# One transformer layer on one core: the MLP's late operand combinations, the second residual and the last row normalization placed elsewhere

## The chip, the cores and the metric

The kernel runs on one core of one Trainium2 chip. The metric is the device time of one execution in microseconds; a time for a kernel is the median of its runs. The profile is one execution, taken by the hardware profiler. Engines are called PE (TensorE), DVE (VectorE), ACT (ScalarE), POOL (GpSimd) and SP (SyncE, whose queue starts most DMAs).

## The reference

One layer of a decoder trunk in float32, with 1024 tokens and a model width of 1024. The first half (token mixing: an HGRN2 branch and a retention branch, merged and projected by `w_o`) is left out here, since the change does not touch it. What follows it:

```python
x = _layer_norm(ALPHA * x + (1 + gate1) * y, ln1_g, ln1_b)       # y: output of w_o
u = x * (1 + scale2) + shift2
h = square(relu(u @ w_up + b_up))                                # 1024 x 4096
y = h @ w_down + b_down                                          # 1024 x 1024
x = _layer_norm(ALPHA * x + (1 + gate2) * y, ln2_g, ln2_b)       # the output
```

`_layer_norm` takes mean and variance over the 1024 columns of a row, normalizes, multiplies by a per-column scale and adds a per-column shift.

## The kernel before

Every float32 matmul is made of three (`mm3`, lines 186 to 188): both operands are split into a high and a low part, and high·high, high·low and low·high are added up in PSUM. A split (`split`, lines 180 to 182) is one ACT copy for the high part and one DVE subtraction for the low part, so each operand costs both engines an operation.

The large products use Strassen's scheme in Winograd's form: a 2x2 block product from seven block products and not eight. Its right-hand combinations for the up projection are T1 to T4, made from the four blocks B11, B12, B21, B22 of `u` (`combos`, line 402): T1 = B12 - B11, T3 = B22 - B12, T2 = B22 - T1, T4 = B21 - T2, computed in place in the float32 blocks (T4 in a tile of its own, tag "tf"), and each split into two tiles of the pool "U" (14 tiles, all in use at this point). Its left-hand combinations S1 to S4 are made from the weights as these are loaded (`specs_S`, line 216; the DVE sums are line 227).

The stages that the change touches, in order:

1. The output projection (`out_proj`, line 1243). For each of eight tiles of 128 tokens: two column halves of 24 matmuls each, then residual and statistics on DVE, `pow` on POOL for the inverse deviation, normalization on ACT (line 1303). One tile later, `out_second` (line 1315) transposes the normalized tile by PE, writes `u`, and makes the second residual `zp = z * RA + RB` (lines 1331 and 1332, 128 x 1024, on DVE), which POOL's queue stores to memory (`z2_d`).
2. `up_plain` (line 1381): the first group of 256 hidden units as four plain products of 24 matmuls, with its outputs squared, combined by DVE and stored from a pool of four "relu" tiles.
3. `combos`, run to its end: T1, then the subtractions for T3, T2, T4, then the splits of T2, T3, T4.
4. `seven` (line 440): the other 15 groups, seven products of 12 matmuls each, in the order A11·B11, S1·T1, S2·T2, S4·B22, S3·T3, the next group's A12·B21, A22·T4. Results leave PSUM through tiles of a pool "e" (14 buffers). `use_square` (line 1350) makes the left-hand combinations of the down projection out of them; POOL's queue stores these (line 1348).
5. `down_seven` (line 1390): the down projection as four stages of 16 steps. A step's operands are split up to five steps ahead (`prepare`). When a piece of 128 x 512 of the output is complete, `first_part` (line 1456) multiplies it by the gate row, adds the second residual (loaded back from `z2_d` by SP into one of three "zp" tiles) and takes the statistics; when both halves of a row tile are there, `second_part` (line 1465) applies mean, deviation, scale and shift in two three-operand DVE operations for each half and stores the half. Row tiles 0 to 3 and the upper halves of 4 to 7 are complete before the last stage is done; the lower halves of 4 to 7 come out of PSUM one after the other at the very end (lines 1493 to 1500).

The order of the instructions on an engine is not the order of the program text. A planner runs the whole program against its own cost estimates and puts next on each engine the instruction that is ready and stands earliest in the text. So a move in the text changes a rank, and an instruction is passed by others while it is not ready. Pools of tiles are laid out like stacks from the left and the right end of the on-chip memory; a pool that opens where another was closed waits until that one's tiles are released.

## Time and profile before

| | us |
|---|---|
| median of 3 runs | 2324.97 |
| lowest, highest | 2318.06, 2326.09 |
| the profiled execution | 2319.84 |
| its span, first to last instruction | 2318.1 |
| PE busy | 2250.6 (97%) |
| DVE busy | 1652.0 (71%) |
| ACT busy | 1008.7 (44%) |
| POOL busy | 294.6 (13%) |
| mean granted clock of PE | 0.994 |

Busy shares are means over stages with different limits. A row of the timeline has a start, a duration, the engine, the line, the operation and the tiles (written <- read), and in brackets the idle time before it with what ended it; rows of operations in a run are merged (x2). A row of the busy time by stretch has the stretch, its length, busy time and instructions for each engine, the granted clock of PE, the DMA share and GB/s. A row of the groups has the line, engine, operation, tiles, shapes and count, then the busy time and the mean of one in ns, then the idle time before them. A row of a single line's instructions has the shortest, median and longest duration in ns, and the first and the last start.

### The profile page before, as it was taken

How to read it: one execution, taken by the hardware profiler on the slowest of the kernel's cores; microseconds unless marked ns; L12 is line 12 of the kernel's file. 1: busy time of each engine (PE TensorE's matmuls, PEld its weight loads, DVE VectorE, ACT ScalarE, POOL GpSimd, SP SyncE). 2: the span in 40 equal slices, each digit the busy share in tenths (PEclk: the TensorE clock that was granted, in tenths of full speed). 3: DMA queues.
4: the chain of work that ended last, by engine and by line, in shares of the span. 5: the costliest groups of instructions: out<-in, count | busy, mean ns of one | idle time of the engine just before them, and what ended most of it. 6: DMA issues, size and time to landing. Idle time of an engine off the chain costs nothing.

```text
span 2318.1 us, 29884 instructions
## 1 busy us (share of the span) xinstructions
PE 2250.6 (97%) x10366; PEld 1851.3 (80%) x10366; DVE 1652.0 (71%) x3078; ACT 1008.7 (44%) x1829; POOL 294.6 (13%) x460
## 2 busy tenths in 40 slices
PE   6999999999999999999989999999989999999997
PEld 5888888888888788778877788888878888788886
DVE  7866768676777556778876667667886666668669
ACT  4433435443333352432435556222465555643441
POOL 0111010111111120010011222013012111100001
PEclk9999999999999999999999999999999999999999
DMA  9676655433333441122234666864244444777653
GB/s 287 220 229 219 224 195 200 159 129 108 116 109 112 164 150 60 42 91 63 75 104 156 236 193 211 297 212 154 95 145 164 154 152 152 283 254 241 211 168 127
DMA packets 227415, 385.86 MB, mean 166 GB/s; under 512 B 17480, under 2 KB 122688, under 8 KB 226496
## 3 DMA queue, kind: packets, MB, share of 16 engines
q1 hardware_dynamic: 197232, 285.95, 38.7%
q0 software_dynamic: 29712, 97.55, 11.3%
q8 instruction: 82, 1.34, 0.2%
q14 instruction: 69, 0.57, 0.1%
q10 hardware_dynamic: 320, 0.45, 0.1%
HBM read 282.17 MB, written 101.72 MB: 166 GB/s over the span
## 4 chain that ended last, share of the span: by engine, by line
PE 62%; issue 23%; DVE 6%; DMA 3%; POOL 3%; ACT 2%; SPq 0%; ACTq 0%; POOLq 0%; DVEq 0%
PE psd L187 11%; PE psd L186 11%; PE psd L188 11%; PE psa L188 3%; PE psa L187 3%; PE psa L186 3%; PE psc L187 3%; PE psc L186 3%; PE psc L188 3%; PE psb L1119 2%; PE psc L1105 1%; PE psb L186 1%; PE psb L187 1%; PE psb L188 1%; DVE U L182 1%
## 5 line engine op out<-in xcount | busy, mean ns | idle before, releaser
L186 PE MATMUL psd<-U,wh 128*128 128x512 f32 x760 | 305.1, 403 | 2.1 <-ACT wh L181 1.5
L187 PE MATMUL psd<-U,wh 128*128 128x512 f32 x760 | 303.8, 400 | 1.4 <-DVE U L182 1.4
L188 PE MATMUL psd<-U,wl 128*128 128x512 f32 x760 | 303.4, 399 | 0.0
L181 ACT ACTIVATE bh<-s 128x512 fp32r<-128x512 f32 x204 | 128.3, 633 | 248.3 <-PE psd L187 61.1
L186 PE MATMUL psd<-U,bh 128*128 128x512 f32 x496 | 193.8, 391 | 2.1 <-DVE e L449 2.1
L188 PE MATMUL psd<-U,bl 128*128 128x512 f32 x496 | 193.7, 390 | 0.0
L187 PE MATMUL psd<-U,bh 128*128 128x512 f32 x496 | 193.5, 390 | 0.0
L182 DVE TENSOR_TENSOR bl<-raw,bh 128x512 fp32r<-128x512 f32 x153 | 104.6, 689 | 121.4 <-ACT bh L181 121.2
L181 ACT ACTIVATE bh<-raw 128x512 fp32r<-128x512 f32 x153 | 96.9, 636 | 216.3 <-PE psd L187 88.8
L182 DVE TENSOR_TENSOR bl<-s,bh 128x512 fp32r<-128x512 f32 x204 | 139.4, 687 | 69.1 <-ACT bh L181 69.1
L186 PEld LDWEIGHTS psd<-U,wh 128*128 128x128 f32 x760 | 143.1, 189 | 31.0 <-ACT U L181 1.9
L187 PEld LDWEIGHTS psd<-U,wh 128*128 128x128 f32 x760 | 143.8, 189 | 28.6 <-DVE U L182 2.8
L188 PEld LDWEIGHTS psd<-U,wl 128*128 128x128 f32 x760 | 144.0, 189 | 27.6 <-DVE wl L182 0.4
L181 ACT ACTIVATE wh<-raw 128x512 fp32r<-128x512 f32 (+1 forms) x87 | 61.7, 730 | 200.5 <-PE psd L187 174.0
L181 ACT ACTIVATE U<-hr 128x512 fp32r<-128x512 f32 x112 | 70.6, 630 | 157.2 <-issue 69.3
L186 PEld LDWEIGHTS psd<-U,bh 128*128 128x128 f32 x496 | 93.6, 189 | 22.2 <-DVE e L449 2.8
L188 PEld LDWEIGHTS psd<-U,bl 128*128 128x128 f32 x496 | 93.4, 188 | 19.6
L187 PEld LDWEIGHTS psd<-U,bh 128*128 128x128 f32 x496 | 93.5, 189 | 19.4
L182 DVE TENSOR_TENSOR U<-hr,U 128x512 fp32r<-128x512 f32 x112 | 76.8, 686 | 44.4 <-ACT U L181 44.0
L186 PE MATMUL psa<-U,bh 128*128 128x512 f32 x248 | 97.7, 394 | 4.6 <-ACT bh L181 4.3
L188 PE MATMUL psa<-U,bl 128*128 128x512 f32 x248 | 97.5, 393 | 1.0 <-DVE bl L182 1.0
L187 PE MATMUL psa<-U,bh 128*128 128x512 f32 x248 | 97.4, 393 | 0.0
(404 smaller groups left out, 5578.1 us busy)
## 6 DMA issues: line engine op xcount, KB each, us to landing
raw<-in_w_in SPq DMA_DIRECT2D x146, 512.0 KB
raw<-in_w_down SPq DMA_DIRECT2D x48, 512.0 KB
raw<-in_w_ada SPq DMA_DIRECT2D x32, 512.0 KB
raw<-in_w_up SPq DMA_DIRECT2D x32, 512.0 KB
raw<-in_w_pb SPq DMA_DIRECT2D x20, 512.0 KB
adw<-in_w_ada SPq DMA_DIRECT2D x16, 512.0 KB
v_d<-e POOLq DMA_DIRECT2D x32, 256.0 KB, 4.4
rg_d<-e POOLq DMA_DIRECT2D x32, 256.0 KB, 2.6
```

The source lines that it names most:

```text
L181: self.nc.scalar.activation(hi, src, AF.Copy)
L182: self.nc.vector.tensor_tensor(lo, src, hi.bitcast(F32), op=ALU.subtract)
L186: r = mm(out, wh, uh, start=start, stop=False, skip_group_check=more)
L187: mm(out, wh, ul, start=False, stop=False, skip_group_check=more)
L188: return r, mm(out, wl, uh, start=False, stop=stop, skip_group_check=more)
L1105: mm(G[e], l[:, n % 2, es], r, start=n == 0 and i == 0, stop=i == 2, skip_group_check=n > 0)
L1119: mm(po, l, r, start=i == 0, stop=i == len(pairs) - 1)
```

## The change

Three edits, and what they need of pools.

- Late combinations: `combos` runs only up to T1's split before the first seven-product group begins. The subtractions for T3, T2, T4 and T2's split come in the text behind the products A12·B21, A11·B11 and S1·T1 of that group; T3's and T4's splits behind S2·T2 and S4·B22. The pool of the temporary and of the "relu" tiles stays open until the last group; "relu" tiles (4) now also hold part of the outputs of the seven-product groups, and "e" has 7 buffers for the rest, where it had 14 for all.
- Second residual: the two operations of 128 x 1024 for each row tile go from DVE to POOL.
- Down projection's normalization: in `first_part` the two operations of a piece that is already in SBUF go to POOL (12 of 16 pieces; the four that come straight from PSUM stay on DVE). In `second_part`, row tiles 0 to 3, and the upper halves of 4 to 6, are normalized by ACT (scale and bias per row, the bias made by a small DVE operation); the column scale is multiplied by DVE (tiles 0 to 3) or POOL (4 to 6), the column shift added by POOL. The lower halves of 4 to 6 and all of 7 stay as they were.

```diff
@@ combos
-        t3 = Bf["B12"]
-        sub(t3, Bf["B22"], t3)
-        t2 = Bf["B22"]
+        t3, t2 = Bf["B12"], Bf["B22"]
+        sub(t3, t2, t3)
         sub(t2, t2, t1)
@@ out_second
-        V.tensor_tensor(zp, z, RA, op=ALU.mult)
-        V.tensor_tensor(zp, zp, RB, op=ALU.add)
+        nc.gpsimd.tensor_tensor(zp, z, RA, op=ALU.mult)
+        nc.gpsimd.tensor_tensor(zp, zp, RB, op=ALU.add)
@@ up_plain
+    def rt(self):
+        return self.tp.tile([P, 512], F32, tag="relu", bufs=4, name=self.uid("relu"))
...
-        tile = lambda: self.tp.tile([P, 512], F32, tag="relu", bufs=4, name=self.uid("relu"))
-        use = self.use_square(0, tile, (1, 1))
+        use = self.use_square(0, self.rt, (1, 1))
@@ down_seven
         def first_part(t, cs, bank=None):
...
-            V.tensor_tensor(z, z if bank is None else bank, consts["g2"][:, cs], op=ALU.mult)
             zp = fp.tile([P, 512], F32, tag="zp", bufs=3, name=self.uid("zp"))
             nc.sync.dma_start(zp, self.z2_d[t][:, cs])
-            V.tensor_tensor(z, z, zp, op=ALU.add)
+            E = nc.gpsimd if bank is None else V
+            E.tensor_tensor(z, z if bank is None else bank, consts["g2"][:, cs], op=ALU.mult)
+            E.tensor_tensor(z, z, zp, op=ALU.add)
             V.bn_stats(stats[:, t, 6 * (cs.start // 512):6 * (cs.start // 512) + 6], z)
 
         def second_part(t):
             mv, rs = self.norm_stats(stats[:, t])
+            nm = stats[:, t, 24:25]
+            if t < 7:
+                V.scalar_tensor_tensor(nm, mv[:, 0:1], -1.0, rs, op0=ALU.mult, op1=ALU.mult)
             for cs in (lo, up):
                 z = rows[t][:, cs]
-                V.scalar_tensor_tensor(z, z, mv[:, 0:1], consts["lg"][:, cs], op0=ALU.subtract, op1=ALU.mult)
-                V.scalar_tensor_tensor(z, z, rs, consts["lb"][:, cs], op0=ALU.mult, op1=ALU.add)
+                if t < 4 or t < 7 and cs == up:
+                    nc.scalar.activation(z, z, AF.Identity, scale=rs, bias=nm)
+                    E = V if t < 4 else nc.gpsimd
+                    E.tensor_tensor(z, z, consts["lg"][:, cs], op=ALU.mult)
+                    nc.gpsimd.tensor_tensor(z, z, consts["lb"][:, cs], op=ALU.add)
+                else:
+                    V.scalar_tensor_tensor(z, z, mv[:, 0:1], consts["lg"][:, cs], op0=ALU.subtract, op1=ALU.mult)
+                    V.scalar_tensor_tensor(z, z, rs, consts["lb"][:, cs], op0=ALU.mult, op1=ALU.add)
                 nc.sync.dma_start(self.out[t * P:(t + 1) * P, cs], z)
@@ build
-    ups = [(("up", j), k.use_square(j, k.et, (1, 0))) for j in range(1, 16)]
+    ups = [(("up", j), k.use_square(j, k.rt, (1, 0))) for j in range(1, 16)]
...
-        with ExitStack() as s:
-            k.tp = k.pool("tf", "right", s)
-            drain(k.second_parts(1))
-            k.up_plain()
-            drain(k.combos(k.u2f, k.tp))
+        k.tp = k.pool("tf", "right", sh)
+        drain(k.second_parts(1))
+        k.up_plain()
+        parts = k.combos(k.u2f, k.tp)
+        for _ in range(4):
+            next(parts)
         sw.close()
         k.hp = k.pool("hparts", "left")
         with ExitStack() as se:
             k.ev = k.pool("ev2", "left", se)
-            k.e_bufs = 14
-            drain(k.seven(ups))
+            k.e_bufs = 7
+            body = k.seven(ups)
+            next(body)
+            for _ in range(3):
+                next(parts)
+            next(body)
+            drain(parts)
+            drain(body)
```

## The prediction

> **What bounds the kernel now.** I read the page's head, then the busy time by stage, then the timeline of the stages in which TensorE is not full.
>
> ```profile
> span 2318.1 us, 29884 instructions
> ```
>
> ```profile
> core 0: us, PE busy (x) PEld busy (x) DVE busy (x) ACT busy (x) POOL busy (x), PEclk, DMA share, GB/s
> 1600.00:1700.00 100.00, 99.25 (x470) 82.33 (x469) 82.19 (x124) 54.27 (x104) 10.41 (x19) 1.00 0.32 106
> 1700.00:1800.00 100.00, 94.68 (x406) 77.38 (x405) 71.23 (x103) 58.76 (x93) 18.11 (x34) 0.97 0.47 157
> ...
> 1712.10:1718.90 6.80, 5.76 (x13) 4.11 (x14) 6.42 (x10) 2.97 (x7) 0.54 (x1) 0.52 0.07 8
> 1718.90:1732.50 13.60, 13.60 (x61) 11.24 (x60) 12.37 (x20) 8.49 (x15) 1.95 (x4) 1.00 0.55 183
> ...
> 1998.00:2002.00 4.00, 4.00 (x11) 3.13 (x12) 4.00 (x7) 2.31 (x5) 1.22 (x3) 0.57 0.74 217
> ...
> 2260.00:2318.00 58.00, 45.05 (x199) 36.94 (x197) 54.75 (x102) 5.88 (x10) 7.85 (x8) 0.92 0.37 127
> ```
>
> In the output projection (1600 to 1700) TensorE idles 0.75 us: nothing is to be won there. Just past 1700 it loses 5.3 us and half its clock for a while. From 2260 on VectorE is busy for 54.75 of 58 us, while TensorE has finished after 45.05, at 2305.05; VectorE alone sets the end. So the change touches one stage with slack and two places that count. Profiled time is 2319.84 us, span 2318.1, so 1.74 us lie around the span.
>
> **The gap at 1708, and the late combinations.**
>
> ```profile
> 1712.15 0.80 PE L186 MATMUL psa<-U,bh 128*128 128x512 f32 x1 [4.33 <-ACT bh L181]
> 1718.69 0.40 PE L186 MATMUL psd<-U,bh 128*128 128x512 f32 x1
> 1997.96 0.50 PE L186 MATMUL psd<-U,bh 128*128 128x512 f32 x1 [2.08 <-DVE e L449]
> ```
>
> ```profile
> 1711.47 0.63 ACT L181 ACTIVATE bh<-s 128x512 fp32r<-128x512 f32 x1 [2.59 <-DVE s L227]
> 1713.79 0.60 ACT L437 ACTIVATE e<-psd 128x512 f32<-128x512 f32 x1 [1.69 <-DVE U L182]
> ```
>
> TensorE finishes A11·B11 at 1712.15 - 4.33 = 1707.8 and waits for the weight combination S1, which VectorE reached only after its work on T2, T3 and T4. The second ACT row shows the first evacuation waiting for VectorE's last such split: the buffer pool that follows reuses the temporary's room. The S1·T1 product then runs 1712.15 to 1718.69 at a granted clock of 0.52, 6.5 us; at full speed a product takes 13.60 / 5 = 2.72 (the five behind it, 1718.90 to 1732.50). Loss: 4.3 + 3.8 = 8.1 us, the most that this edit can return.
>
> After it, S1, S2, S4 and S3 stand ahead of the three subtractions, so S1·T1 starts at 1707.8 and ends at 1710.5; the next in program order, S2·T2, needs T2. What is late next is VectorE:
>
> ```profile
> L182 DVE TENSOR_TENSOR U<-U,U 128x1024 fp32r<-128x1024 f32 x10 | 11.8, 1218 | 0.0
> L408 DVE TENSOR_TENSOR U<-U,U 128x1024 f32<-128x1024 f32 x6 | 7.1, 1216 | 0.0
> ```
>
> ```profile
> 1686.19 2.35 DVE L408 TENSOR_TENSOR U<-U,U 128x1024 f32<-128x1024 f32 x2
> 2297.53 1.28 DVE L1462 TENSOR_TENSOR row<-row,zp 128x512 f32<-128x512 f32 x2
> 2313.51 1.41 DVE L1470 SCALAR_TENSOR_TENSOR row<-row,stats,lb 128x512 f32<-128x512 f32 x2
> ```
>
> These pairs give the cost in a queue: 2.35 - 1.22 = 1.13 us for 1024 columns, 1.28 - 0.68 = 0.60 for 512, 1.41 - 0.74 = 0.67 for the three-operand form. From 1686.2 to the first half of T2's low part stand 15 operations of 1024 columns (2 for T1, 4 low parts of B12 and B22, 2 of T1, 6 subtractions, 1 of T2) and 16 of 512 (two weight low parts, four S sums and their low parts, the next group's A12, four of the plain product's output, one sum): 17.0 + 9.6 = 26.6, and 2.3 for a GpSimd lock (below): 1715.1. TensorE can fill with the next group's A12·B21 (to 1713.3) and S4·B22 (to 1716.0). Both fills: no wait, -8.1. One: 1.8 idle. What does such an idle cost? The 2.08 us at 1996 was followed by 4 us at a clock of 0.57, 1.7 us more; so 3.5 in all, -4.6. None: 4.6 idle and 3.8 of slow clock as now, about 0. I take -6.4, midway between the first two, as the planner picks what is ready.
>
> The Trainium skill ("TensorE: Matmul & The Clock Gate", Why this matters for your kernels) warns only of idle gaps beyond about 3 us; by it one fill would leave -6.3 and not -4.6. The 2.08 us row speaks against it, and I go by the row.
>
> Fewer "e" buffers cost nothing in my count: a group now needs six from seven, and four from "relu"; the products of a group, 7 times 2.72 = 19 us, cover the time in which an output waits for its store. Without that cover each late evacuation would stop TensorE.
>
> **Second residual on GpSimd.**
>
> ```profile
> L1331 DVE TENSOR_TENSOR zp<-z,RA x8: 1220/1226/1226, 1610.4 to 1683.8; 128x1024 f32<-128x1024 f32 x8
> ```
>
> ```profile
> 1696.98 0.69 ACT L1358 ACTIVATE relu<-psd,cols 128x512 f32<-128x512 f32 x1 [0.65 <-PE psd L188]
> ```
>
> This multiply and an addition like it leave VectorE, eight times. Now the row of this trace that matters most, GpSimd's 128x512 tensor_tensor in the projection before, first on GpSimd, then what VectorE did beside it:
>
> ```profile
> 1571.46 2.20 POOL L1221 TENSOR_TENSOR U<-U,e 128x512 f32<-128x512 f32 x1 [0.63 <-DVE U L1220]
> 1576.15 1.28 POOL L1221 TENSOR_TENSOR U<-U,e 128x512 f32<-128x512 f32 x1 [2.49 <-DVE U L1220]
> ```
>
> ```profile
> 1571.31 1.21 DVE L182 TENSOR_TENSOR wl<-raw,wh 128x1024 fp32r<-128x1024 f32 x1
> 1572.55 2.19 DVE L182 TENSOR_TENSOR wr<-raw,wr 128x1024 fp32r<-128x1024 f32 x1
> ...
> 1575.99 0.68 DVE L1218 TENSOR_TENSOR U<-U,psd 128x512 f32<-128x512 f32 x1
> 1576.71 1.28 DVE L1220 TENSOR_TENSOR U<-U,e 128x512 f32<-128x512 f32 x1
> ```
>
> Alone it takes 1.28. When a VectorE operation with both inputs in SBUF is running, GpSimd waits for its end (1572.5) and ends at 1573.66; the next VectorE operation of that kind waits for that (1572.55 to 1574.74, 1.1 past GpSimd's end). L1220 likewise ends 0.56 after GpSimd's 1577.43. L1218, with one input in PSUM, keeps its 0.68, and GpSimd keeps its 1.28 beside it. So the two engines exclude each other for operations with two inputs in SBUF: moving one takes 0.60 off VectorE and can block VectorE for 1.14 (1572.52 to 1573.66).
>
> A 1024-column operation on GpSimd has no row. It lies between 1.28 and twice that, 2.6; I take 2.3, near the upper end, for little of the 1.28 is fixed if it goes as VectorE's 0.68 and 1.22. Two per row tile are 4.6 of a period of (1683.8 - 1610.4) / 7 = 10.5 us, on an engine 10% busy (10.41 of 100): hidden under the next tile's 48 matmuls. Only the last tile counts: the multiply (from 1683.8) ends about when T1's subtraction starts at 1686.2, the addition gets in between, and that chain moves by 2.3. T1's subtraction then ends at 1688.5 + 2.3 = 1690.8 and the first half of B12's low part at 1692.0. The third plain product ends at 1696.9 (the ACT row above) and lasts two products, 5.4, so it starts near 1691.5: +0.5, between -0.7 (all the idle time of 1600 to 1700) and +2.3 (all of the shift). The tile's store leaves 2 x 2.3 - 2 x 1.23 = 2.1 us later; pow and the next store queue behind it on GpSimd, the next buffer pool waits for it, and two plain products cover that.
>
> **The normalization of the down projection.**
>
> ```profile
> L1470 DVE SCALAR_TENSOR_TENSOR row<-row,stats,lb 128x512 f32<-128x512 f32 x16 | 11.3, 744 | 0.0
> L1469 DVE SCALAR_TENSOR_TENSOR row<-row,stats,lg 128x512 f32<-128x512 f32 x16 | 11.2, 742 | 0.0
> L1462 DVE TENSOR_TENSOR row<-row,zp 128x512 f32<-128x512 f32 x12 | 7.9, 682 | 0.0
> L1463 DVE BATCH_NORM_STATS2 stats<-row 128x6 f32<-128x512 f32 x12 | 7.9, 681 | 0.0
> L182 DVE TENSOR_TENSOR U<-U,U 128x512 fp32r<-128x512 f32 x8 | 5.5, 684 | 0.0
> L1459 DVE TENSOR_TENSOR row<-row,g 128x512 f32<-128x512 f32 x8 | 5.3, 680 | 0.0
> L182 DVE TENSOR_TENSOR U<-hr,U 128x512 fp32r<-128x512 f32 x7 | 4.6, 661 | 0.0
> ```
>
> ```profile
> L1240 POOL TENSOR_TENSOR stats<-stats,small 128x1 f32<-128x1 f32 x8 | 7.8, 981 | 298.8 <-DVE stats L1239 298.8
> ```
>
> From 2257 VectorE loses 16 operations of the first parts (8 pieces), 16 three-operand ones of rows 0 to 3 against 8 multiplies, and 6 of rows 4 to 6: 9.6 + 10.7 - 4.8 + 4.0 = 19.5 us off. ScalarE gets 11 at 0.63 (the bh row above) = 6.9, beside TensorE's last products. GpSimd gets 16 + 8 + 6 = 30, at 1.28 each 38.4. What counts is what the two share. VectorE keeps 15 splits, 4 zp sums and 8 multiplies at 0.60 and 10 three-operand ones at 0.67 with two inputs in SBUF: 16.2 + 6.7 = 22.9. Together 61.3 us from 2257.2: 2318.5, where VectorE's last operation now ends at 2314.92. So +3.5; each GpSimd operation holds VectorE only 1.14 of its 1.28, and I leave those 4 us for operations that don't fit into one another.
>
> The bounds. Below, no exclusion: then row 7 alone follows TensorE's end, three first-part operations, pow at 0.98 and four three-operand ones, 1.8 + 1.0 + 2.7 = 5.5: 2310.5, -4.4. Above, nothing of GpSimd's work rides under VectorE's: 38.4 - 19.5 = +18.9. What can ride are VectorE's 12 statistics, 8 sums from PSUM and 4 products from PSUM, 24 x 0.60 = 14.4.
>
> That statistics operations, with one SBUF input, ride free is taken from L1218; if not, 7.2 of the 14.4 go. The Trainium skill ("SBUF — State Buffer", Who interferes with whom) bears on that: the lock is exclusive, and a VectorE instruction with at most one SBUF input does not contend; no row here has a statistics operation beside GpSimd.
>
> Four first parts move at 2088 too: 8 x 1.28 = 10.2 of GpSimd for 4.8 taken off, over splits made five steps of 2.72 ahead, which cover the difference: 0. On SP's queue their zp loads wait for a GpSimd sum and the next weight load stands behind; without the five steps that would be 5 us.
>
> **Sum.** 2319.84 - 6.4 + 0.5 + 3.5 = 2317.4, that is -2.4; on the median of the runs, 2324.97 (5.1 above the profiled execution), 2322.6.
>
> **Rivals.** (1) GpSimd's work overlaps after all, the tail ends 4.4 earlier: -6.4 + 0.5 - 4.4 = -10.3, 2314.7. For it: TensorE is done at 2305 and VectorE's load falls by 19.5. Against: the four rows of VectorE beside GpSimd. (2) The gap stays: VectorE's groups of 1686 to 1714 show no idle time and only their order changes; if the planner's order leaves TensorE without a fill, 0 + 0.5 + 3.5 = +4.0, 2329.0. Against: S4·B22 needs nothing of T2. (3) Slower: VectorE takes its queue in order and stands at the first operation that is blocked, so that little rides under GpSimd, and the last splits come late.
>
> ```profile
> 2292.55 0.69 DVE L182 TENSOR_TENSOR U<-U,U 128x512 fp32r<-128x512 f32 x1
> 2293.50 0.40 PE L187 MATMUL psd<-U 128*128 128x512 f32 x1
> ```
>
> The last split ends at 2293.24 and its matmul starts at 2293.50: 0.26 us of room, then TensorE waits too. If half of the 14.4 rides, the tail is 18.9 - 7.2 = 11.7 longer: -6.4 + 0.5 + 11.7 = +5.8, 2330.8. It decides the sign once less than 13.0 of the 14.4 rides (18.9 - 13.0 = 5.9, the gain of the rest).
>
> **Chances.** Forecast 0.50 (its own range 2317 to 2328), (1) 0.18, (2) 0.14, (3) 0.15, else 0.03. The range that holds 8 of 10 goes from 2310 (rival 1 with both fills, -8.1 + 0.5 - 4.4 = -12.0, and the lower part of the runs' spread of 8 us) to 2335 (rival 3 with one fill, -4.6 + 0.5 + 11.7 = +7.6, and the upper part). About 0.5%, 11.6 us, is what a measurement of this kernel tells from no change: faster than that 0.14 (most of rival 1's lower half and a little of the forecast), slower 0.11 (rival 3 with little riding, or with 2), within 0.75.
>
> **What would show it.** The wait at 1712 with its 0.52 clock gone, S1·T1 directly behind A11·B11, and S4·B22 or the next A12·B21 ahead of S2·T2: edit one right. A tail in which GpSimd's L1221-like durations go from 1.28 to 2 and more and VectorE's multiplies and splits stretch past 0.7: the lock. If these stay short and the time from TensorE's end to the span's falls from 13.05 to some 8.7 us, I am wrong on the largest term. TensorE waiting for VectorE in its last twenty microseconds would be rival 3.

## The result, and the profile after

The change makes the kernel slower by little: 2328.50 us (2324.86 to 2333.13, 18 runs) after, against 2320.73 us (2315.02 to 2326.09, 18 runs) before on the same chip. The ratio is 1.0035 with a 95% interval of 1.0028 to 1.0043, so 6.5 to 10.0 us more, 8.1 in the middle. The forecast was 2.4 us less. The time lies in the range of 2310 to 2335 and within the 0.5% called no change, but just above the forecast's own 2317 to 2328; the sign is the other one.

The profiled execution after takes 2329.25 us, its span is 2327.1. Its busy time by stretch (columns as before):

```profile
core 0: us, PE busy (x) PEld busy (x) DVE busy (x) ACT busy (x) POOL busy (x), PEclk, DMA share, GB/s
1600.00:1700.00 100.00, 94.60 (x440) 77.73 (x439) 80.21 (x99) 48.34 (x96) 51.71 (x32) 0.98 0.33 111
1700.00:1800.00 100.00, 98.12 (x431) 80.43 (x430) 79.72 (x111) 62.02 (x99) 18.92 (x35) 1.00 0.45 156
2260.00:2327.00 67.00, 47.01 (x207) 38.27 (x205) 51.36 (x82) 15.35 (x23) 49.65 (x38) 0.88 0.33 113
```

Three things have changed. The hole behind 1700 is nearly closed: PE is busy 98.12 of 100 us there and not 94.68. A hole has opened in the output projection, which had none: 94.60 and not 99.25. And in the tail DVE has less work (51.36 us in 67, where it had 54.75 in 58) but needs longer for it: it now waits.

To see how much each is worth, the span is cut at three events that every version has: the start of the first (A) and of the last transposes (B) of the output projection, and the first DVE sum of the tail (C). These are the rows of before at A, B and C, from its timeline of PE and of DVE:

```profile
1607.05 1.09 PE L1325 MATMUL psa<-cst,z 128*128 128x128 f32 x8
...
1683.81 1.09 PE L1325 MATMUL psa<-cst,z 128*128 128x128 f32 x8 [0.61 <-ACT z L1303]
...
2257.22 1.28 DVE L1477 TENSOR_TENSOR row<-row,psa 128x512 f32<-128x512 f32 x2
```

And of after, with the start of S1·T1 (1718.08), the next group's A12·B21 (1721.03) and the two waits of PE that are left between B and C:

```profile
1611.01 1.09 PE L1324 MATMUL psa<-cst,z 128*128 128x128 f32 x8 [0.40 <-ACT z L1302]
...
1692.62 1.15 PE L1324 MATMUL psa<-cst,z 128*128 128x128 f32 x8 [4.21 <-ACT z L1302]
...
1718.08 0.39 PE L186 MATMUL psa<-U,bh 128*128 128x512 f32 x1
...
1721.03 0.39 PE L186 MATMUL psc<-U,bh 128*128 128x512 f32 x1
...
1724.59 0.50 PE L186 MATMUL psa<-U,bh 128*128 128x512 f32 x1 [1.82 <-ACT e L436]
...
1999.94 0.50 PE L186 MATMUL psd<-U,bh 128*128 128x512 f32 x1 [0.74 <-DVE e L448]
...
2258.95 1.28 DVE L1488 TENSOR_TENSOR row<-row,psa 128x512 f32<-128x512 f32 x2
```

The same cut for every kernel run below, each from its own profiled execution (us), beside what the runs say of the whole (in e8, e10 and e14 C is the first product from a bank, since the sum comes later there):

| kernel | A | A to B | B to C | C to end | median of runs | against before, ratio (95%) |
|---|---|---|---|---|---|---|
| before | 1607.05 | 76.76 | 573.41 | 60.88 | 2320.73 | |
| after | 1611.01 | 81.61 | 566.33 | 68.15 | 2328.50 | 1.0035 (1.0028 to 1.0043) |
| e1_late | 1608.07 | 76.76 | 563.61 | 60.86 | 2311.13 | 0.9972 (0.9961 to 0.9983) |
| e2_zp | 1608.46 | 81.69 | 572.86 | 60.79 | 2326.61 | 1.0031 (1.0020 to 1.0043) |
| e3_tail | 1610.28 | 76.75 | 571.20 | 67.57 | 2327.63 | 1.0043 (1.0031 to 1.0055) |
| e4_late_tail | 1606.61 | 76.76 | 563.66 | 67.97 | 2320.39 | 1.0004 (0.9995 to 1.0012) |
| e5_psum | 1611.07 | 77.64 | 574.31 | 60.78 | 2325.39 | 1.0033 (1.0020 to 1.0046) |
| e6_first | 1607.99 | 76.75 | 573.17 | 64.69 | 2322.41 | 1.0024 (1.0014 to 1.0033) |
| e7_second | 1607.87 | 76.75 | 570.95 | 65.23 | 2323.37 | 1.0024 (1.0013 to 1.0035) |
| e8_best | 1613.33 | 76.76 | 566.40 | 60.61 | 2313.62 | 0.9982 (0.9970 to 0.9993) |
| e9_six | 1607.10 | 82.31 | 574.84 | 60.85 | 2329.38 | 1.0044 (1.0032 to 1.0057) |
| e10_tail8 | 1609.77 | 76.75 | 566.78 | 58.30 | 2311.50 | 0.9966 (0.9953 to 0.9978) |
| e11_late_tail8 | 1610.38 | 76.76 | 565.41 | 60.75 | 2313.91 | 0.9973 (0.9962 to 0.9984) |
| e12_psum7 | 1606.63 | 77.94 | 571.27 | 60.86 | 2320.25 | 1.0012 (1.0003 to 1.0021) |
| e13_first_zp8 | 1607.81 | 76.76 | 570.72 | 64.11 | 2322.39 | 1.0008 (0.9999 to 1.0017) |
| e14_relu5 | 1608.48 | 76.76 | 565.61 | 58.35 | 2310.97 | 0.9965 (0.9952 to 0.9977) |

How to read it. Where the code of the stretch is the old one, A to B and C to the end repeat to 0.1 us (A to B: 76.75 or 76.76 in eleven kernels; C to the end: 60.78 to 60.88 in six), so they can be compared row by row. A lies between 1606.6 and 1613.3 although no edit touches what runs before it (but for two operations of each row tile in e5 and e12), and the B to C stretch of the old code (before, e3, e6, e7, e13) goes from 570.7 to 573.4: these two are differences between executions, so a single profile doesn't tell less than 7 us in A nor less than 3 us in B to C. For B to C the profiles show where most of it comes from. PE pauses near 1998 in each of the five, and behind the pause of before (2.08 us) and of e6 (2.00) the granted clock is 0.58 and 0.57 for 4 us, while behind those of e3, e7 and e13 (1.40, 1.67 and 1.73) it stays at 1.00. Before and e6 are the two of 573, the others the three of 571. So before's own profile has some 2 us that other executions of the same code don't have. Of after's 9.0 us more in span, 4.0 are A, and the rest is +4.85 in the output projection, -7.1 in the products, +7.3 in the tail.

### The profile page after: what moved, and what is told of

Its sections match the earlier page's. It is cut to its first block, busy times and chain, and to the rows that moved or that the text cites. A ratio compares the mean times of both kernels' runs of the same rounds, so it can differ in the third digit from the quotient of the medians.

```text
span 2327.1 us, 29910 instructions
## 1 busy us (share of the span) xinstructions
PE 2253.1 (97%) x10366; PEld 1853.2 (80%) x10366; DVE 1649.0 (71%) x3031; ACT 1015.5 (44%) x1840; POOL 390.1 (17%) x514
## 4 chain that ended last, share of the span: by engine, by line
PE 48%; issue 33%; DVE 6%; POOL 5%; DMA 5%; ACT 2%; SPq 0%; ACTq 0%; POOLq 0%; DVEq 0%
PE psd L187 9%; PE psd L186 9%; PE psd L188 9%; PE psa L187 2%; PE psa L186 2%; PE psa L188 2%; PE psb L1118 2%; PE psc L187 2%; PE psc L186 2%; PE psc L188 2%; PE psc L1104 1%; DVE U L182 1%; DMA z_d<-zp 1%; PE psb L186 1%; PE psb L188 1%
## 5 line engine op out<-in xcount | busy, mean ns | idle before, releaser
L182 DVE TENSOR_TENSOR bl<-raw,bh 128x512 fp32r<-128x512 f32 x153 | 104.5, 688 | 117.4 <-ACT bh L181 117.1
L182 DVE TENSOR_TENSOR bl<-s,bh 128x512 fp32r<-128x512 f32 x204 | 138.8, 685 | 65.9 <-ACT bh L181 65.9
L182 DVE TENSOR_TENSOR U<-hr,U 128x512 fp32r<-128x512 f32 x112 | 78.7, 703 | 37.8 <-ACT U L181 37.7
```

The lines of the kernel that those rows point to most:

```text
L182: self.nc.vector.tensor_tensor(lo, src, hi.bitcast(F32), op=ALU.subtract)
```

## The experiments

The kernels of e1 to e4 ran beside one another and beside before (2319.01 us there), and so did e5 to e8 (2318.53), e9 to e11 (2318.96), e12 (2317.33), e13 and e14 (2320.40). Each has 5 to 12 runs. A difference in us is the ratio in the table less one, times before's median beside it; across these groups the ratios compare, the medians don't.

### One edit at a time: e1, e2, e3, e4

e1 has the late combinations with their pools and nothing else, e2 the second residual alone, e3 the normalization alone; e4 is the whole change with the second residual left on DVE:

```diff
@@ e4: out_second of the kernel after
-        nc.gpsimd.tensor_tensor(zp, z, RA, op=ALU.mult)
-        nc.gpsimd.tensor_tensor(zp, zp, RB, op=ALU.add)
+        V.tensor_tensor(zp, z, RA, op=ALU.mult)
+        V.tensor_tensor(zp, zp, RB, op=ALU.add)
```

> Only the late combinations (and what they need of pools); second residual and normalization as before. Theory (the loss of the whole change comes from the two moves to GpSimd): TensorE's wait at the first seven-product group and the slow clock behind it go, -7 us against before, about 2314. Rival (the rearranged group and its fewer buffers cost elsewhere what they bring, and the gain seen in the whole change belongs to the shifted start): within 2 us of before.

> Only the second residual on GpSimd. Theory (VectorE's two-input operations wait out GpSimd's 2.4 to 2.7 us operations, the last tile has no cover): VectorE's three-operand operation of line 1297 or 1298 lasts 2.9 and not 0.69 where it meets one, TensorE waits about 4 us for the last tile's transposes, +5 us against before. Rival (GpSimd is idle enough, and the +4.9 seen there needs the late combinations beside it): +0.5, no wait over 1.6 us at the transposes.

> Only the normalization of the down projection shared by the three engines. Theory (exclusion of VectorE and GpSimd, and the last row tiles in series): +7 us against before, all of it between the first sum of the up half near 2257 and the end; TensorE's end moves by under 1 us, and from there to the span's end it takes 19 to 20 us and not 13. Rival (the tail of the whole change was long because its planner's order followed another start): between -4 and +2.

> The whole change with the second residual left on VectorE. Theory (the three edits add up: -7, +5, +7): about 0 against before, 8 us below the sum of the whole change's +7.8 minus nothing else, so +1 to +3. Rival (they don't add, the late combinations gain less once the second residual is back in VectorE's chain): +5 or more.

In the runs e1 is 6.5 us faster than before (3.9 to 9.0), e2 7.2 slower (4.6 to 10.0), e3 10.0 slower (7.2 to 12.8), e4 0.9 slower (-1.2 to +2.8). The table puts each in its own stretch, and the others move by no more than executions differ: e1 in B to C, e2 in A to B (+4.93), e3 in C to the end (+6.7). So the change is a gain of some 7 us and two losses of some 7, and the second residual, costed at next to nothing, is what turns the sign: without it (e4) the change is even.

e1's profile shows what is left of the hole at 1708. The row of its PE timeline at the first group and DVE's at the same place:

```profile
1714.35 0.50 PE L186 MATMUL psa<-U,bh 128*128 128x512 f32 x1 [0.97 <-ACT e L436]
...
1710.03 0.69 DVE L1371 TENSOR_TENSOR relu<-relu,relu 128x512 f32<-128x512 f32 x1 [1.29 <-DMA h_d0L<-relu]
```

Its busy time by stretch:

```profile
1700.00:1800.00 100.00, 98.97 (x436) 81.32 (x435) 76.52 (x111) 61.26 (x98) 18.93 (x35) 1.00 0.47 161
```

PE is busy 98.97 of 100 us at a clock of 1.00 (before: 94.68 at 0.97), and the only wait there is one of 0.97 us, behind DVE, which stood 1.29 us at a "relu" tile still waiting for its store.

### Why the second residual costs 7 us: e5, e9, e12

After's own rows show the place. First POOL, then DVE, from the timeline around the last two row tiles:

```profile
1683.00 2.40 POOL L1330 TENSOR_TENSOR zp<-z,RA 128x1024 f32<-128x1024 f32 x1 [1.55 <-ACT z L1302]
1685.47 2.72 POOL L1331 TENSOR_TENSOR zp<-zp,RB 128x1024 f32<-128x1024 f32 x1
...
1684.20 1.74 DVE L182 TENSOR_TENSOR wl<-raw,wh 128x512 fp32r<-128x512 f32 x1
1685.87 2.88 DVE L1297 SCALAR_TENSOR_TENSOR z<-xt,z 128x512 f32<-128x512 f32 x1
...
1694.15 5.27 DVE L408 TENSOR_TENSOR U<-U,U 128x1024 f32<-128x1024 f32 x2 [2.92 <-ACT U L1327]
```

DVE's last sum for `z` of tile 7 (L1297, two inputs in SBUF) takes 2.88 us and not 0.69, since it stands until tile 6's addition on POOL ends at 1688.2. `z` is then late, and PE waits 4.21 us for it. T1's two subtractions meet tile 7's POOL operations in the same way: 5.27 us and not 2.35.

e5 keeps the second residual on POOL and takes away what is blocked: the gate product stays in PSUM, so that both operations of `z`'s chain have one input in SBUF.

```diff
@@ e5: out_proj of e2
-                V.tensor_tensor(z[:, cs], po, g1[:, cs], op=ALU.mult)
-                V.scalar_tensor_tensor(z[:, cs], xt[:, cs], ALPHA, z[:, cs], op0=ALU.mult, op1=ALU.add)
+                V.tensor_tensor(po, po, g1[:, cs], op=ALU.mult)
+                V.scalar_tensor_tensor(z[:, cs], xt[:, cs], ALPHA, po, op0=ALU.mult, op1=ALU.add)
```

> Second residual on GpSimd as in the run that made that edit alone, but the gate product of the output projection stays in PSUM, so that the two-operation chain that makes z on VectorE has one input in SBUF in each of its operations. Theory (the exclusion of two-SBUF-input operations delays z's chain): the residual operation keeps about 0.7 us beside GpSimd instead of 2.88, TensorE's wait at the last transposes falls from 4 us to at most 1.5 us, the output projection is again 78 to 80 us long instead of 83.2, and the time is within +1 us of the kernel before or a little below it. Rival (the order of pow, store and additions on GpSimd, or the store, makes the delay): the wait stays near 4 us and the time 5 to 7 us above the kernel before.

Its timeline, DVE and then PE:

```profile
1684.16 0.68 DVE L1298 SCALAR_TENSOR_TENSOR z<-xt,psd 128x512 f32<-128x512 f32 x1
...
1690.24 5.32 DVE L408 TENSOR_TENSOR U<-U,U 128x1024 f32<-128x1024 f32 x2 [2.92 <-ACT U L1328]
...
1688.71 1.09 PE L1325 MATMUL psa<-cst,z 128*128 128x128 f32 x8 [1.24 <-ACT z L1303]
...
1719.43 0.79 PE L186 MATMUL psa<-U,bh 128*128 128x512 f32 x1 [6.30 <-ACT bh L181]
```

The sum beside POOL's 2.39 and 2.40 us takes 0.68, PE's wait falls from 4.21 to 1.24, and the projection is 77.64 us long: each as the theory said. The Trainium skill ("SBUF — State Buffer", Who interferes with whom) says that a VectorE instruction with at most one input in SBUF stays out of the lock; the 0.68 beside 2.88 bears that out. But the time hardly falls: 7.7 us above before (4.6 to 10.7), where at most 1 was expected. Part of the stall has only gone on: T1's subtractions still take 5.32 us, the combinations behind them come late, and the hole at 1708 grows from 4.33 to 6.30 us. The stretch B to C is 1 to 4 us longer than the old code's, the stretch A to B 0.9; about 3 us of the middle value lie in no stretch behind A, and A is 4 us later in that execution.

e9 tries the other reading, that only the last two tiles matter: tiles 0 to 5 on POOL, 6 and 7 on DVE.

```diff
@@ e9: out_second of e2 (e12 makes the same edit with t < 7, on e5)
-        nc.gpsimd.tensor_tensor(zp, z, RA, op=ALU.mult)
-        nc.gpsimd.tensor_tensor(zp, zp, RB, op=ALU.add)
+        E = nc.gpsimd if t < 6 else V
+        E.tensor_tensor(zp, z, RA, op=ALU.mult)
+        E.tensor_tensor(zp, zp, RB, op=ALU.add)
```

> Second residual on GpSimd for row tiles 0 to 5 only; tiles 6 and 7 keep it on VectorE. Theory (a delayed z costs nothing while enough products are queued in front of its transposes, and only the last two tiles lack that cover): the output projection from its first to its last transposes is 77 to 78.5 us long, TensorE's wait there is 1 us or less, the gap at 1708 stays 4 to 5 us, and the time is within 1.5 us of the kernel before. Rival (every tile on GpSimd costs something, by the lock on weight splits or otherwise): 3 to 6 us above the kernel before.

It is, beside e3, the slowest of all, 10.2 us above before (7.4 to 13.2), and its projection is the longest, 82.31 us. The timeline says how, DVE and then PE:

```profile
1665.66 2.89 DVE L1298 SCALAR_TENSOR_TENSOR z<-xt,z 128x512 f32<-128x512 f32 x1
1668.47 3.42 DVE L182 TENSOR_TENSOR U<-U,U 128x1024 fp32r<-128x1024 f32 x1
...
1679.21 1.22 DVE L1332 TENSOR_TENSOR zp<-z,RA 128x1024 f32<-128x1024 f32 x1 [1.31 <-ACT z L1303]
...
1681.61 0.68 DVE L1297 TENSOR_TENSOR z<-psd,g 128x512 f32<-128x512 f32 x1
...
1689.41 1.97 PE L1325 MATMUL psa<-cst,z 128*128 128x128 f32 x8 [4.75 <-ACT z L1303]
```

Tile 5's operations on POOL block tile 6's `z` (2.89) and a split (3.42), so tile 6 is late; its residual on DVE is then ready only at 1679.2, and `z` of tile 7 stands behind it in the queue. A delay of one tile is handed to the next, since the 48 matmuls of a tile cover PE and not DVE's order. My theory that a covered tile costs nothing is wrong.

e12 joins the two: e5 with the last tile's residual on DVE.

> Second residual on GpSimd for row tiles 0 to 6 with the gate product kept in PSUM, and the last tile's residual on VectorE, ahead of T1's subtractions as in the kernel before. Theory (two things cost in the output projection: the three-operand sum of z's chain with two SBUF inputs, behind GpSimd, and T1's subtractions behind the last tile's GpSimd operations): both are gone, the output projection is 77 to 78.5 us from its first to its last transposes, the gap at 1708 is 4 to 5 us instead of 6.3, and the time is within 2 us of the kernel before. Rival (a cost that does not show in these two places, such as the transfer of the residual or the run-up to the output projection): still 4 us or more above the kernel before.

```profile
1684.57 1.09 PE L1325 MATMUL psa<-cst,z 128*128 128x128 f32 x8 [1.28 <-ACT z L1303]
...
1712.62 0.50 PE L186 MATMUL psa<-U,bh 128*128 128x512 f32 x1 [4.03 <-ACT bh L181]
```

In these two rows of its PE timeline the wait at the transposes is as short as in e5, and the hole at 1708 is back to its old size. The time is 2.8 us above before (0.7 to 4.9), a little more than the 2 expected; e2, beside its own runs of before, was at 7.2 (4.6 to 10.0). So the middle values say that two blocked places make most of the loss, the three-operand sum of `z`'s chain and T1's subtractions; the intervals overlap a little. In e2 itself the second is hidden behind the first: its wait at 1720 for S1 is 3.98 us, no longer than before's 4.33, and grows only in e5. With both out of the way POOL's seven tiles still gain nothing: PE, busy for 99.25 of 100 us in this stretch of before, sets the pace there, and not DVE.

### Why the tail is 7 us longer and not 3.5: e6, e7, e13

e6 has only the first parts on POOL, e7 only the shared second part:

```diff
@@ e6: first_part of before
-            V.tensor_tensor(z, z if bank is None else bank, consts["g2"][:, cs], op=ALU.mult)
...
-            V.tensor_tensor(z, z, zp, op=ALU.add)
+            E = nc.gpsimd if bank is None else V
+            E.tensor_tensor(z, z if bank is None else bank, consts["g2"][:, cs], op=ALU.mult)
+            E.tensor_tensor(z, z, zp, op=ALU.add)
@@ e7: second_part of before
...
+                if t < 4 or t < 7 and cs == up:
+                    nc.scalar.activation(z, z, AF.Identity, scale=rs, bias=nm)
+                    E = V if t < 4 else nc.gpsimd
+                    E.tensor_tensor(z, z, consts["lg"][:, cs], op=ALU.mult)
+                    nc.gpsimd.tensor_tensor(z, z, consts["lb"][:, cs], op=ALU.add)
...
```

> Of the tail's edit only the first parts that start from a kept row are on GpSimd; the second part is as before. Theory (what rides under VectorE is less than counted, phase by phase): the phase up to row 0's reciprocal root grows by about 2.3 us and the rest keeps its length, so +2 to +3 us. Rival (the first parts cost nothing, the sharing of the second part has all of the loss): within 1 us of the kernel before.

> Of the tail's edit only the second part is shared between ScalarE, VectorE and GpSimd; the first parts stay on VectorE. Theory: rows 0 to 3 lose about 2.7 us and rows 4 to 7 about 2.2 us, so +4 to +5.5 us. Rival (the loss comes from the first parts and only shows later): within 1.5 us of the kernel before.

e6's tail is 3.8 us longer, e7's 4.35; together 8.2, and both at once (e3) 6.7. In the runs each is 5.6 us slower (3.2 to 7.7 and 3.0 to 8.1). For e6 that is above the 2 to 3 expected, for e7 at the upper end of 4 to 5.5; neither half is free. After's profile has both. DVE's waits in its tail (engine, tile and line waited for; sum, times, longest), where before has none:

```profile
DVE stats L1465 <- POOL row L1464: 8.3, 5, 3.1
DVE stats L1471 <- POOL stats L1239: 3.2, 5, 1.5
```

And the rows behind them, from the timeline of DVE, of SP's queue and of ACT:

```profile
2271.16 0.69 DVE L1465 BATCH_NORM_STATS2 stats<-row 128x6 f32<-128x512 f32 x1 [3.05 <-POOL row L1464]
...
2275.51 1.15 DVE L182 TENSOR_TENSOR U<-hr,U 128x512 fp32r<-128x512 f32 x1
...
2308.37 1.44 DVE L1464 TENSOR_TENSOR row<-row,zp 128x512 f32<-128x512 f32 x1
...
2312.07 0.16 DVE L1471 SCALAR_TENSOR_TENSOR stats<-stats 128x1 f32<-128x1 f32 x1 [0.44 <-POOL stats L1239]
...
2312.81 0.68 DVE L1463 TENSOR_TENSOR row<-psd,g 128x512 f32<-128x512 f32 x1
...
2317.96 0.68 DVE L1463 TENSOR_TENSOR row<-psb,g 128x512 f32<-128x512 f32 x1
...
2262.41 17.44 SPq L1461 DMA_DIRECT2D zp<-z_d  x7
2279.94 0.38 SPq L1409 DMA_DIRECT2D hr<-h_d13L  x1
...
2266.88 0.64 ACT L181 ACTIVATE U<-hr 128x512 fp32r<-128x512 f32 x1 [2.49 <-PE psb L188]
```

In the first part POOL's 16 operations run in a row for 21.5 us, and DVE's statistics, which were to ride beside them, wait for their results: 8.3 us of idle time. DVE had work that was ready: ACT has made its half of the next four left splits by 2267.5, and DVE's half of the first comes only at 2275.51, since it stands behind the statistics in the queue. The planner's order and not the data keeps DVE idle there. (The left operands after these do come late, at 2279.94 and not 2271.70 as before: their loads stand behind the seven residual loads on SP.) In the last rows the period is 2317.96 - 2312.81 = 5.15 us: each row gives two three-operand operations away and gets back a blocked addition (1.44 and not 0.69), a wait of 0.44 for the bias, and a chain one row at a time, where before DVE took rows in pairs (2296.11 to 2305.59 for two, 4.74 each).

Is it SP's queue or POOL's own time? e13 is e6 with eight buffers for the reloaded residual:

```diff
@@ e13: first_part of e6
-            zp = fp.tile([P, 512], F32, tag="zp", bufs=3, name=self.uid("zp"))
+            zp = fp.tile([P, 512], F32, tag="zp", bufs=8, name=self.uid("zp"))
```

> The first parts from kept rows on GpSimd, as in the run that made that edit alone, but eight buffers for the reloaded second residual and not three, so that no such load waits in SP's queue in front of the left operands' loads. Theory 1 (SP's queue makes the loss: the left operands come 8 us late, and the last splits with them): the long stretch of SP disappears, TensorE's wait of 2.4 us for a split at 2296 goes, and of the 3.8 us that the tail gained in length at least 2.5 go: within 1.5 us of the kernel before. Theory 2 (GpSimd's 16 operations of 1.25 to 1.30 in a row, 20 us, with the statistics behind them, make it): the tail stays 3 us or more longer, 3 to 5 us above the kernel before.

Its SP timeline:

```profile
2258.75 7.93 SPq L1460 DMA_DIRECT2D zp<-z_d  x4
2271.89 0.32 SPq L1408 DMA_DIRECT2D hr<-h_d13L  x1
```

Its waits of DVE and of PE (columns as above):

```profile
DVE stats L1464 <- POOL row L1463: 7.2, 5, 3.0
...
PE psd L187 <- DVE U L182: 1.8, 1, 1.8
```

The long stretch is gone and the load comes at 2271.89, where it stood before the change (2271.70). The tail gets 0.6 us shorter, 64.11 us, still 3.2 above 60.88; DVE's wait for POOL is 7.2 where e6 had 8.3, PE's wait for a split goes from 2.4 to 1.8. The runs, 1.9 us above before (-0.2 to +3.9), lie between the two expectations. The tail's length speaks for POOL's own serial time, with SP's queue as the smaller part. The runs alone don't decide it: e6 was at 5.6 (3.2 to 7.7), and by the middle values the loads could be worth more than 0.6.

### What the tail is really bound by: e8, e10, e11, e14

If DVE sets the end, work should be moved out of the tail in time and not to another engine. e8 is e1 with the upper halves' kept parts multiplied by the gate row and joined with the residual one stage earlier, on DVE, so that the last bank needs only a product and a sum:

```diff
@@ e8: down_seven of e1
+        def early(t):
+            z = rows[t][:, up]
...
+            V.tensor_tensor(z, z, consts["g2"][:, up], op=ALU.mult)
+            V.tensor_tensor(z, z, zp, op=ALU.add)
+        def late(t, bank):
...
+            V.tensor_tensor(y, bank, consts["g2"][:, up], op=ALU.mult)
+            def rest():
+                z = rows[t][:, up]
+                V.tensor_tensor(z, z, y, op=ALU.add)
+                V.bn_stats(stats[:, t, 6:12], z)
...
@@ e10 and e11: on e8 and on e1
-DOWN_TAIL = 6
+DOWN_TAIL = 8
```

> Late combinations alone, and in the down projection the upper halves' kept part gets its gate product and second residual ahead of the last seven products, on VectorE, so that after the last bank only a product, a sum and the statistics are left. This takes 8 operations of 512 columns, 8 x 0.60 = 4.8 us, out of VectorE's last 60 us. Theory (VectorE's queue sets the end of the tail): the tail from 2257 on is 4 to 5 us shorter, and the time about 11 to 12 us below the kernel before. Rival (the end is set by the order of the last row's work behind TensorE's end): no more than 1 us below the run with the late combinations alone, so 7 to 8 us below the kernel before.

The tail stays as long as it was, 60.61 us, so the theory is wrong and the rival right about the end. The time is 4.2 us below before (1.6 to 7.0), less even than the rival's 7 to 8. DVE's timeline shows where the 4.8 us went:

```profile
2293.11 0.69 DVE L1460 TENSOR_TENSOR row<-psd,g 128x512 f32<-128x512 f32 x1 [2.46 <-PE psd L188]
...
2298.25 0.69 DVE L1460 TENSOR_TENSOR row<-psd,g 128x512 f32<-128x512 f32 x1
```

DVE is early and waits 2.46 us for row 4's bank; from then on it needs 2298.25 - 2293.11 = 5.14 us for each row, alone and no longer in a pair. Most of the rest of the gain went there. (5.14 with everything on DVE beside after's 5.15: for a row by itself, sharing the work with ACT and POOL brought nothing.) e10 and e11 make the last four banks finish farther apart:

> Late combinations and the early gate product and residual of the upper halves, as in the run before, and the products of the last eight steps instead of six are taken row by row at the end, so that the last four rows' banks finish 8 x 0.69 = 5.5 us apart instead of 4.1. Theory (VectorE needs 5.14 us for each of the last four rows, one after the other, from the moment row 4's bank is ready; in the run before it waited 2.46 us for that bank): row 4's bank comes earlier, VectorE's wait for it goes, and the span from TensorE's end to the end falls from 11.8 to 9.5 or less; 9 to 12 us below the kernel before. Rival (the weight parts of two more steps are held and the splits come late): TensorE waits for VectorE or ScalarE in the last 60 us and the time is no better than in the run before, 5 us below the kernel before.

> Late combinations, and the last eight steps instead of six taken row by row, without the early part. Theory (VectorE has a backlog of its own up to the last four rows here and waits for no bank): the tail keeps its length, 7 to 9 us below the kernel before, as with the late combinations alone. Rival (the order of the banks alone sets the end): 2 us or more below that.

e10's tail is 58.30 us, 2.6 shorter than before's, 9.5 of it behind PE's end, and its DVE goes on without a wait (its timeline):

```profile
2286.04 1.41 DVE L1491 SCALAR_TENSOR_TENSOR row<-row,stats,lb 128x512 f32<-128x512 f32 x2
2287.37 0.68 DVE L1460 TENSOR_TENSOR row<-psd,g 128x512 f32<-128x512 f32 x1
```

e11, the same stagger without the early part, stays at 60.75: without room on DVE an earlier bank is worth nothing. Both tails are as expected. In the runs e10 is 7.9 us below before (5.1 to 10.9; 9 to 12 expected), e11 6.3 (3.7 to 8.8; 7 to 9 expected), so e10's gain over e1's 6.5 is seen in its profile only.

e14 gives e10 a fifth "relu" tile (and six "e" tiles, not seven):

> The kernel with late combinations, early upper halves and eight steps row by row, with five tiles and not four for the outputs that wait for their stores (and six for the rest, not seven). Theory (VectorE stands 1.3 to 3.0 us at an output whose tile still waits for its store, and TensorE's wait of 1.0 to 2.7 us in the first group follows from it): that wait and VectorE's are gone, and the time is 1.5 to 4 us below the kernel with four tiles, 9 to 12 us below the kernel before. Rival (the wait only moves to the next bank): TensorE still waits 1 us or more there and the time is as with four tiles, 7 to 8 us below the kernel before.

DVE's wait for a store is 0.94 us here where e10 had 3.04, and PE's wait in the first group 1.06 us and not 2.73 (the rows of its DVE and PE timeline):

```profile
1710.69 0.69 DVE L1376 TENSOR_TENSOR relu<-relu,relu 128x512 f32<-128x512 f32 x1 [0.94 <-DMA h_d0L<-relu]
...
1713.95 0.50 PE L186 MATMUL psa<-U,bh 128*128 128x512 f32 x1 [1.06 <-ACT e L436]
```

So the store does set that wait, but it is not gone, and PE waits 2.6 us elsewhere between B and C (0.9 in e10). The time, 8.1 us below before (5.3 to 11.1), can't be told from e10's: the rival's case, and not the 9 to 12 of the theory. e10 and e14 have the lowest ratios of all runs; both beat the kernel before and the kernel after, but their intervals overlap those of e1 and e11.

## Why the prediction went wrong

**The gap at 1708 (-6.4): right.** The rows of after show what was named: S1·T1 begins at 1718.08 directly behind A11·B11, the next group's A12·B21 at 1721.03, ahead of all but one matmul of S2·T2, and the wait of 4.33 us with its clock of 0.52 is gone. In the runs e1 returns 6.5 us; in the profiles the B to C stretch is 563.6 to 566.8 us in the five kernels with the late combinations, four "relu" tiles and the residual on DVE (e1, e4, e8, e10, e11), against 570.7 to 573.4 of the old code, 6.7 between the means. That -6.4 was hit so closely is in part luck. It is the middle between both fills without a wait (-8.1) and one fill with 1.8 us of it (-4.6); e1 shows both fills begun ahead of the bulk of S2·T2, a wait of 0.97 us for another reason, and a shorter pause near 1990 (0.65 us, where before had 2.08 and a slow clock behind it) that was in no sum. One step in it was wrong: "Fewer "e" buffers cost nothing". The cover of 19 us holds for "e", but the four "relu" tiles now take the next outputs while the stores of the first group are still under way, and PE waits 0.6 to 2.7 us for it. Another was right for another reason: the 1.8 us of idle time that one fill would leave is there (1.82 at 1724.59), but for that store and not for T2.

**Second residual (+0.5): this step turned the sign.** It read "hidden under the next tile's 48 matmuls. Only the last tile counts". Those matmuls hide POOL's own time from PE. They don't hide it from DVE, whose queue makes the next tile's `z` from the next tile's first products on. I had the rule (two inputs in SBUF exclude each other), its price (an operation on POOL can hold DVE for its whole length) and its victim in T1's chain, and did not list the other victims on DVE in that time: L1298, L182. The listing can be made from DVE's timeline of before, at tile 6:

```profile
1673.43 1.23 DVE L1331 TENSOR_TENSOR zp<-z,RA 128x1024 f32<-128x1024 f32 x1 [1.31 <-ACT z L1303]
...
1676.31 0.69 DVE L1298 SCALAR_TENSOR_TENSOR z<-xt,z 128x512 f32<-128x512 f32 x1
```

With 2.4 us for each, POOL's second operation would run from about 1675.9 to 1678.3 (an estimate from after's rows). The three-operand sum of the next `z` falls 0.4 us into it and waits out 2 us, with no slack behind it, since PE waits for the last `z` by 0.61 us already before. That is part of what was measured; the rest is handed on from the tiles ahead: after's DVE has the 2.89 and the 3.42 us of e9 too, at 1669.39 and 1672.20. Measured: 4.21 us of PE's wait, 4.9 us in the stretch up to B, behind B a clock of 0.65 (after) and 0.50 (e2) over the next 3 us, and 7.2 us in the runs of e2. The estimate of 2.3 us for 1024 columns was close (2.40, beside DVE 2.72 to 3.26).

**The tail (+3.5): right in kind, half in size.** The sum let the two engines exclude each other and nothing else: 61.3 us from the first sum to DVE's last operation. It took 2323.93 - 2258.95 = 65.0. The term that was mis-sized is the 14.4 us that "can ride": DVE's statistics have one SBUF input and indeed run at 0.69 beside POOL, but they read what POOL is just making, and DVE takes its queue in order. 11.5 us of idle time (8.3 and 3.2) stand where there was none. Read in that sum, 3.7 of the 14.4 did not ride (65.0 less 61.3). That is the mechanism of rival 3, which put half of the 14.4 as lost and the tail at +11.7, and had a chance of 0.15; the measured +7.3 is between forecast and rival. The sign that rival 3 was to show, PE waiting for DVE in its last twenty microseconds, is absent in after (PE waits 0.6 us in its whole tail) and present in e6 (2.41 us at 2296). The listed signs of the lock came, if weaker: DVE's multiplies and splits stretch to as much as 1.79 us, POOL's operations to 1.77 and not to 2, and from PE's end at 2307.65 to the end of the span it is 19.45 us, where it was 13.05 before and 8.7 would have proved me wrong. SP's queue, which the prediction looked at for 2088 only, matters in the tail too, by 0.6 us in the profiles of e6 and e13.

**The sum.** -6.4 + 0.5 + 3.5 = -2.4 was predicted. One edit at a time the runs give -6.5 (e1), +7.2 (e2), and +0.9 for the first and the third together (e4), so +7.4 for the third: -6.5 + 7.2 + 7.4 = +8.1, as measured. (The third alone, e3, is at +10.0, but its profiled execution has 3.2 of it ahead of A and 6.7 in the tail.) The edits add up within the 2 to 3 us that each interval leaves; the error is 6.7 in the second and 3.9 in the third.

What stays open: some 3 us of e5's time, and whether the kernels' different starts (A) are chance alone. They come from before the output projection, where every version has the same code. The clock has a share in them: near 800 PE pauses for 2.92 us in before and for 2.91 us in e1, at the same instruction, and over the 4 us behind it the granted clock is 1.00 in before and 0.59 in e1.

## What to carry to other kernels

Before an elementwise operation is given to GpSimd, list VectorE's operations with two inputs in SBUF that run in that time, and look for the one that the next stage waits for: moving 512 columns takes 0.60 us off VectorE and held it here for up to 1.1 (a split of 1.78 us and not 0.68), so a busy VectorE can pay more than it gains. Count as riding beside GpSimd only what doesn't read GpSimd's result, and remember that an engine stops at the first instruction that is blocked. When an engine bounds the tail, moving its work to an earlier stage, with the last banks finishing farther apart (e10), made the tail 2.6 us shorter where moving it to another engine made it longer; in the whole time e10 can't be told from e1. And before a cost of an edit is read from two profiles, look whether the clock fell behind the same pause in both.

## What was not expected of the hardware

- The granted clock can fall behind pauses of PE of about 2 us, but the length of the pause alone doesn't decide it. From the last transposes to the end of the span, a clock of 1.00 stayed at 1.00 behind pauses of up to 1.87 us (e14; 1.82 in after), and behind 2.00 (e6), 2.08 (before), 2.41 (e6), 2.66 (e8), 2.73 (e10) and each of 3.8 us and more it was at 0.50 to 0.73 over the next 2 us. Two other rows don't fit an edge between them: behind 1.75 us in before the clock is 0.64 over 4 us, and behind 2.67 us in e11 it stays at 1.00. From the timeline of PE and the busy time by stretch, before and then e11:

```profile
990.41 0.62 PE L911 MATMUL psb<-cst,e 128*128 128x128 f32 x2 [1.75 <-ACT e L903]
...
990.41:994.41 4.00, 4.00 (x16) 3.68 (x16) 1.43 (x3) 0.83 (x3) 0.60 (x1) 0.64 0.27 100
...
1718.36 0.50 PE L186 MATMUL psa<-U,bh 128*128 128x512 f32 x1 [2.67 <-ACT e L436]
...
1718.36:1724.36 6.00, 5.93 (x25) 4.57 (x26) 6.00 (x7) 4.86 (x6) 0.54 (x1) 1.00 0.44 142
```

The Trainium skill ("TensorE: Matmul & The Clock Gate", Why this matters for your kernels) warns of gaps of more than about 3 us; here gaps of 1.75 to 2.91 us were followed by a slow clock in some executions and not in others. What else decides it no run here shows. So the prediction's price for one fill, 1.8 us idle and 1.7 of slow clock behind it, is what such a pause can cost and not what it must: behind the 1.82 us of after there was no slow clock.

- Where GpSimd's operation and VectorE's meet, GpSimd's is longer by less than 1 us (2.40 to between 2.72 and 3.26 in after's output projection, 1.28 to at most 1.77 in its tail), while VectorE's waits out what is left of GpSimd's (0.69 to 2.88 us): most of the cost of the exclusion falls on VectorE here. It holds for the smallest operations too: a VectorE operation on one column took 1.25 us there and not 0.16 (after, at 2290.35).
